# A two-layer decoder trunk on eight cores: earlier token loads, a longer prologue, another order of chunk steps, and a last group in two halves

## The chip, the cores and the metric

The kernel runs on the 8 cores of one Trainium2 chip. Every core computes one of eight batch elements, with the same program. The metric is device microseconds of the slowest core. Some executions fall into a slow state (the cores of one die at a lower granted TensorE clock, the time 2 to 19% longer in the runs here). Ratios and intervals here use fast runs alone; the medians of times in the tables are over all runs, slow ones included.

## The reference, cut to what matters

```python
def reference(x, ...):                       # x: (8, 2048, 1024) float32, one batch element a core
    for i in range(2):
        h = rmsnorm(x, norm_mix_g[i])
        x = x + (mlstm_mixer if i == 0 else gla_mixer)(h, ...)   # 4 heads, dk 128, dv 256
        h = rmsnorm(x, norm_ffn_g[i])
        x = x + square(relu(h @ w1[i])) @ w2[i]                  # 1024 -> 4096 -> 1024
    return rmsnorm(x, final_norm_g)
# mlstm_mixer: q, k, v, output gate and input/forget gates are one projection of h; a recurrence over
# chunks with a matrix state C (dk x dv a head) and a vector state n; a norm by head; a projection out.
```

## The kernel before

The tokens are on the free axis: `xT` is [128 partitions, 8 blocks of 128 features, 2048 tokens]. They are taken in four groups of 512 and sixteen chunks of 128. The program does not issue its instructions directly. It records them as units with the tiles that they read and write. A list scheduler then orders each engine's queue by a model of times, and the order that comes out is emitted. So a change of the recording order or of a dependency can move any instruction.

```python
    def order(s):                          # the scheduler, cut
        ...
        for e in s.E:                      # each engine: the unit of its window that can start first
            cand = []
            for n in todo[e][:s.WIN[e]]:
                ...                        # rdy: when its predecessors are done in the model
                st = max(free[e], rdy)
                cand.append((st, n))
```

The square sums of RMSNorm have two forms. The direct one sends each of eight squares through TensorE (eight matmuls against ones). The other one adds four squares on GpSimd first, so that TensorE gets only two matmuls a group.

```python
    def sq_half(g, hf):                    # four of the eight feature blocks of group g
        for i, k in enumerate(ks):
            act(sq[:, i % 2, :], xT[:, k, tgs(g)], AF.Square, ...)
            if i == 1:   tt(sd[:], sq[:, 0, :], sq[:, 1, :], ALU.add, ..., 512, "pool")
            elif i == 2: tt(sd[:], sd[:], sq[:, 0, :], ALU.add, ..., 512, "pool")
            elif i == 3: tt(sqb[:, hf, :], sd[:], sq[:, 1, :], ALU.add, ..., 512, "pool")

    def xn_op(layer, g, gcol, k):          # x * gain * rstd on VectorE: two operands from SBUF
        stt(XN[...], xT[:, k, tgs(g)], gains[...], rstd[:], ALU.mult, ALU.mult, ...)
```

One chunk of a mixer. S2 is the output (scores times values plus query times state), P2a to P2c the norm by head, S34 the state update, Cst the bf16 copy of the state, S7 the transposition of a chunk's result, S1 the next chunk's scores. `f()` takes one of the chunk's fills: projections of later chunks and groups, the output projection, statistics of the next group.

```python
                s.S2(i)
                s.P2a(i)
                s.S34(i, 0)
                s.S34(i, 1)
                s.Cst(i)
                f()
                if i > 0:
                    s.S7(i - 1)
                f()
                s.P2b(i)
                s.P2c(i)
```

The loads of the start and the prologue (cut):

```python
    for k0 in range(0, KC, 2):
        load_x("sp", 0, k0, 2)                      # token group 0, hardware queue
    load_cols(wqk, "wqk", m_win_d, 0, 2)            # q/k weights, cast to bf16 on the software queue
    load_z(0)                                       # weights of the input and forget gates
    load_cols(wv, "wv", m_win_d, 1024, 4)
    load_cols(wo, "wo", m_win_d, 2048, 4)
    load_x("pool", 1, 0, 8)                         # token group 1
    stats_direct(0, range(KC), MB)                  # group 0; group 1 follows in chunk 0, by GpSimd
    ...                                             # q/k of group 0, gates, values of chunks 0 to 3
    wout_load(0, 0)
    load_x("pool", 2, 0, 8)
```

The last group of the kernel is one block of 512 columns: down projection, add, square, statistics, and then eight outputs of 512 columns with their stores.

## Time and profile before

| | before |
|---|---|
| time, first four runs (one of them slow) | 1529.52 us median |
| time, all 16 runs (five of them slow) | 1529.0 us median, 1527.28 to 1671.56 |
| time, the 11 fast runs | 1528.7 us mean |
| profiled spans of the cores | 1520.0 to 1526.2 us |
| priced TensorE work | 1429.0 us |
| the rest ("excess"), slowest core | 97.2 us |

Excess is the measure of the prediction, which says how each matmul is priced: the wall time less the priced TensorE work. It rises only where TensorE stands or runs at a low clock. Where I give it for stretches below, it is the mean of the six cores whose traces are complete (cores 2 and 4 lack some matmul records, which inflates theirs).

The busy line of the page of before gives for each engine busy microseconds, share of the span, and instructions:

```profile
PE 1461.7 (96%) x7476; PEld 688.8 (45%) x7476; DVE 807.2 (53%) x1433; ACT 603.2 (40%) x1245; POOL 186.8 (12%) x173
```

The waits of TensorE in before (who waited <- who ended the wait: total us, times, longest):

```profile
PE ps L230 <- ACT sq L236: 19.9, 4, 9.0
PE ps L230 <- DVE hn L240: 7.8, 1, 7.8
PE ps L230 <- DVE R L244: 4.7, 7, 1.2
PE ps L230 <- DMA wv<-m_win: 3.3, 1, 3.3
```

These few waits hold over a third of the excess, and the change aims at them. Two groups of VectorE (line, engine, operation, tiles, shapes, count | busy us, mean ns of one | idle time before them):

```profile
L244 DVE SCALAR_TENSOR_TENSOR xn<-xT,gains,rstd 128x512 bf16<-128x512 f32 x128 | 96.2, 791 | 28.8 <-ACT rstd L236 28.7
...
L244 DVE SCALAR_TENSOR_TENSOR tiny<-tiny 128x4 f32<-128x4 f32 x32 | 7.5, 235 | 2.2 <-ACT junk L236 0.6
```

A group of GpSimd (POOL):

```profile
L240 POOL TENSOR_TENSOR sd<-sq 128x512 f32<-128x512 f32 x36 | 46.5, 1291 | 530.4 <-ACT sq L236 353.6 <-DVE NB L608 159.5 <-ACT rstd L236 17.3
```

An operation on 4 columns that means 235 ns, where its neighbours of the same size on the timeline take 160, and an xn that means 791, where an undisturbed one takes 737 to 753, are the trace of something that holds VectorE back some of the time. (The 0.69 us of the prediction is the spacing of xn in a row: two take 1.40.) The single records are plainer than the means: 10 of the 128 xn take over 0.76 us, up to 1.85, and each of these lies beside a GpSimd sum; none of the 113 that lie beside no sum does, not even the 7 beside a DMA issue of GpSimd. The timeline of before at the 7.8 us hole shows it (start us, duration us, engine, line, operation, tiles, shapes, count, idle before <- releaser):

```profile
71.08 2.80 DVE L724 TENSOR_SCALAR Cbf<-R,egs 128x256 bf16<-128x256 f32 x4
...
71.72 0.71 POOL L190 DMA_DIRECT2D wst<-m_wout  x1 [59.37 <-DVE Cbf L724]
...
72.44 1.28 POOL L240 TENSOR_TENSOR sd<-sq 128x512 f32<-128x512 f32 x1
...
74.58 1.26 POOL L240 TENSOR_TENSOR sd<-sd,sq 128x512 f32<-128x512 f32 x1 [0.86 <-ACT sq L236]
...
74.88 0.99 DVE L240 TENSOR_TENSOR n<-n,egs 128x4 f32<-128x4 f32 x1
```

Four state copies took 2.80 us here (by the single records three took 0.35 us each and the last 2.01, to 0.16 us after the end of the first sum), and a product of 4 columns 0.99 us, up to the end of a GpSimd sum that had begun 0.3 us before it.

### The profile page before, as it was taken

The page shows a single profiled execution, that of the slowest core. Times are in us where ns is not written, and L with a number is a line of the kernel's source. Part 1 is how long each engine was busy: PE and PEld are TensorE (multiplying, and loading weights), DVE is VectorE, ACT ScalarE, POOL GpSimd, SP SyncE. Part 2 cuts the span into 40 slices and gives each one's busy share as a digit, 9 for nine tenths or more (in the row PEclk, how much of TensorE's full clock was granted, in tenths as well). Part 3 has the DMA queues.
Part 4 walks back from the last instruction along what each step waited for, and adds up shares of the span by engine and source line. Part 5 has one row for each costly group of instructions (what it writes and reads, how often), then busy time and mean ns, then how long its engine had stood idle before and what let it go on. Part 6 is the DMA issues. An engine that isn't in the chain of part 4 may idle for free.

```text
span 1526.2 us, 22507 instructions; the slowest of 8 cores (1520.0 to 1526.2 us)
## 1 busy us (share of the span) xinstructions
PE 1461.7 (96%) x7476; PEld 688.8 (45%) x7476; DVE 807.2 (53%) x1433; ACT 603.2 (40%) x1245; POOL 186.8 (12%) x173
## 2 busy tenths in 40 slices
PE   4789999999999999999999999999999999999996
PEld 1345454544444444444444544444444444444442
DVE  1276563875433434434557876768743443343367
ACT  1667676663013013013255866677410310301333
POOL 2030101322000000000110201034200000000042
PEclk9989999999999999999999999999999999999998
DMA  9920000373321330330301100036430331200014
GB/s 153 262 84 1 2 1 1 56 112 56 56 35 22 56 52 4 56 56 1 55 1 56 56 1 1 1 56 95 73 55 3 54 56 21 36 1 1 1 56 166
DMA packets 35697, 72.87 MB, mean 48 GB/s; under 512 B 4336, under 2 KB 4336, under 8 KB 35584
## 3 DMA queue, kind: packets, MB, share of 16 engines
q0 software_dynamic: 29104, 60.87, 23.0%
q1 hardware_dynamic: 6480, 10.57, 2.1%
q8 instruction: 62, 1.02, 0.3%
q14 instruction: 51, 0.42, 0.1%
HBM read 109.23 MB, written 8.39 MB: 77 GB/s over the span
## 4 chain that ended last, share of the span: by engine, by line
PE 85%; DVE 4%; ACT 3%; issue 3%; DMA 3%; POOL 1%; DVEq 0%; ACTq 0%; POOLq 0%; another core or an unknown queue 0%
PE ps L230 84%; DMA wv<-m_win 3%; ACT og L236 1%; DVE oT L244 1%; PE ps L744 1%; DVE R L244 1%; POOL sd L240 1%; DVE xn L244 1%; DVE xT L240 1%; ACT hnT L236 1%; ACT sq L236 1%; ACT junk L236 0%; PE ps L633 0%; DVE ps L240 0%; POOL sqb L240 0%
## 5 line engine op out<-in xcount | busy, mean ns | idle before, releaser
L230 PE MATMUL ps<-xn,w1b 128*128 128x512 bf16 x2048 | 445.1, 379 | 0.0
L230 PE MATMUL ps<-hid,w2b 128*128 128x512 bf16 x1920 | 417.0, 379 | 0.0
L236 ACT ACTIVATE rt<-ps 128x512 f32<-128x512 f32 x256 | 152.8, 597 | 604.9 <-PE ps L230 599.4
L240 DVE TENSOR_TENSOR xT<-ps,xT 128x512 f32<-128x512 f32 x320 | 219.3, 688 | 245.9 <-PE ps L230 245.7
L230 PEld LDWEIGHTS ps<-xn,w1b 128*128 128x128 bf16 x2048 | 200.2, 98 | 239.7
L240 DVE TENSOR_TENSOR hid<-rt 128x512 bf16<-128x512 f32 x240 | 172.1, 718 | 224.1 <-ACT rt L236 223.9
L230 PEld LDWEIGHTS ps<-hid,w2b 128*128 128x128 bf16 x1920 | 187.9, 98 | 226.2
L236 ACT ACTIVATE sq<-xT 128x512 f32<-128x512 f32 (+1 forms) x160 | 96.8, 623 | 100.4 <-DVE xT L240 47.0
L230 PE MATMUL ps<-wv,xn 128*128 128x512 bf16 x512 | 120.6, 382 | 3.4 <-DMA wv<-m_win 3.3
L230 PE MATMUL ps<-wo,xn 128*128 128x512 bf16 x512 | 120.8, 384 | 1.4 <-ACT vt L236 0.6
L230 PE MATMUL ps<-xn,wqk 128*128 128x512 bf16 x512 | 118.1, 383 | 2.5 <-DVE xn L244 2.5
L230 PE MATMUL ps<-hnT,wout 128*128 128x512 bf16 x512 | 117.8, 382 | 2.0 <-ACT vt L236 2.0
L244 DVE SCALAR_TENSOR_TENSOR xn<-xT,gains,rstd 128x512 bf16<-128x512 f32 x128 | 96.2, 791 | 28.8 <-ACT rstd L236 28.7
L240 POOL TENSOR_TENSOR sd<-sq 128x512 f32<-128x512 f32 x36 | 46.5, 1291 | 530.4 <-ACT sq L236 353.6
L236 ACT ACTIVATE og<-og 128x512 f32<-128x512 f32 x128 | 80.6, 629 | 12.4 <-ACT og L236 1.5
L230 PEld LDWEIGHTS ps<-xn,wqk 128*128 128x128 bf16 x512 | 49.8, 99 | 61.4 <-issue 6.2
L230 PEld LDWEIGHTS ps<-wo,xn 128*128 128x128 bf16 x512 | 49.4, 99 | 60.7 <-issue 8.1
L230 PEld LDWEIGHTS ps<-hnT,wout 128*128 128x128 bf16 x512 | 49.1, 98 | 57.7 <-issue 5.1
L230 PEld LDWEIGHTS ps<-wv,xn 128*128 128x128 bf16 x512 | 48.8, 98 | 56.5 <-issue 6.9
L244 DVE SCALAR_TENSOR_TENSOR R<-R,egs,ps 128x256 f32<-128x256 f32 x120 | 57.2, 477 | 15.7 <-PE ps L230 9.0
L236 ACT ACTIVATE junk<-ps 128x256 bf16<-128x256 f32 x128 | 48.6, 379 | 18.7 <-DVE ps L240 6.2
L240 POOL TENSOR_TENSOR sd<-sd,sq 128x512 f32<-128x512 f32 x36 | 47.5, 1320 | 66.4 <-ACT sq L236 62.2
(121 smaller groups left out, 987.7 us busy)
## 6 DMA issues: line engine op xcount, KB each, us to landing
w1b<-w POOLq DMA_DIRECT2D x16, 1024.0 KB, 15.8
w2b<-w POOLq DMA_DIRECT2D x16, 1024.0 KB, 14.3
outT<-oT SPq DMA_DIRECT2D x16, 512.0 KB, 2.9
xT<-xT POOLq DMA_DIRECT2D x3, 2048.0 KB, 65.6
wst<-m_wout POOLq DMA_DIRECT2D x4, 1024.0 KB, 9.0
wst<-g_wout POOLq DMA_DIRECT2D x4, 1024.0 KB, 5.6
xT<-xT SPq DMA_DIRECT2D x4, 512.0 KB, 10.1
wqk<-m_win POOLq DMA_DIRECT2D x4, 512.0 KB, 19.2
```

The source lines that it names most:

```text
L230: t.op("pe", lambda e: e.matmul(out, lhsT=lhsT, rhs=rhs, start=start, stop=stop), r=r, w=w, sig=sig, ns=max(cols, 150) * (1.7 if f32 else ...
L236: t.op("act", lambda e: e.activation(out=out, in_=in_, func=func, **kw), r=r, w=w, ns=190 + 0.84 * n + (190 if acc is not None else 0))
L240: t.op(eng, lambda e: e.tensor_tensor(out=out, in0=in0, in1=in1, op=op), r=r, w=w, ns=170 + 1.03 * n if eng == "dve" else 200 + 2.2 * n)
L244: t.op("dve", lambda e: e.scalar_tensor_tensor(out=out, in0=in0, scalar=scalar, in1=in1, op0=op0, op1=op1), r=r, w=w, ns=200 + 1.07 * n)
L744: t.op("pe", lambda e, h=h, e2=e2, e8=e8: e.transpose(tpS[:, e8, :], in_=hn[:, h, e2 * 128:(e2 + 1) * 128], identity=ident[:]), r=[("hn", ...
```

## The change

The intent: TensorE has no projection to do for the first 25 us and waits for VectorE and ScalarE in the first chunks. So both first token groups are loaded ahead of the weights, more work that needs no state is done before the first chunk, group 1's normalisation leaves the first chunks, the chunk's steps are ordered so that TensorE finds something to do between the norm's steps, and the last group's statistics are hidden behind outputs of its first half.

The diff, cut to its core (the list of fills and the index arithmetic of the tail are left out):

```diff
@@ the scheduler: a queue's transfers keep their order
+                held = False
                 for n in todo[e][:s.WIN[e]]:
+                    if s.units[n]["dma"]:
+                        if held:
+                            continue
+                        held = True
@@ the fills of a chunk, first mixer: values two chunks ahead
+            v = s.v(i + 2) if i + 2 < NCH and not (s.m and i < 2) else []
+            o = s.o(i + 1) if i + 1 < NCH else []
...
@@ the steps of a chunk, first mixer only
                 s.S2(i)
                 s.P2a(i)
-                s.S34(i, 0)
-                s.S34(i, 1)
-                s.Cst(i)
-                f()
-                if i > 0:
-                    s.S7(i - 1)
-                f()
-                s.P2b(i)
-                s.P2c(i)
+                    if i > 0:
+                        s.S7(i - 1)
+                    s.S34(i, 0)
+                    s.P2b(i)
+                    s.S34(i, 1)
+                    s.P2c(i)
+                    s.Cst(i)
+                    f()
@@ loads and prologue
+    load_x("sp", 1, 0, 4)
+    load_x("sp", 1, 4, 4)
-    load_cols(wqk, "wqk", m_win_d, 0, 2)
-    load_z(0)
-    load_cols(wv, "wv", m_win_d, 1024, 4)
-    load_cols(wo, "wo", m_win_d, 2048, 4)
-    load_x("pool", 1, 0, 8)
+    load_cols(wqk, "wqk", m_win_d, 0, 2, after=[("xT", 0, 1)])
+    load_z(0, [("xT", 0, 1)])
+    load_cols(wv, "wv", m_win_d, 1024, 2, after=[("wqk", 2)])
+    load_cols(wo, "wo", m_win_d, 2048, 2, after=[("wv", 2)])
...
+    for k in range(4):
+        slab(k)                                     # q/k of group 0, six outputs
+        stats_direct(1, (2 * k, 2 * k + 1), 7)      # group 1's statistics, direct
...
+    qk1 = m0.qk(1, 0) + m0.qk(1, 1)                 # half of group 1's q/k, before the first chunk
@@ output weights later
-    hooks.setdefault(0, []).extend([(3, lambda: wout_load(0, 1))])
-    hooks.setdefault(1, []).extend([(1, lambda: wout_load(0, 2)), (5, lambda: wout_load(0, 3))])
-    hooks.setdefault(2, []).extend([(3, lambda: load_x("pool", 3, 0, 8))])
+    hooks.setdefault(0, []).extend([(4, lambda: wout_load(0, 0))])
+    hooks.setdefault(1, []).extend([(1, lambda: wout_load(0, 1)), (4, lambda: wout_load(0, 2))])
+    hooks.setdefault(2, []).extend([(1, lambda: wout_load(0, 3)), (3, lambda: load_x("pool", 3, 0, 8))])
@@ the last token group in two halves of 256 columns
+    for hf in range(2):
+        for j in range(KC):
+            ...                                     # down projection, add, square, statistics in bank 6 + hf
+        ...                                         # Ln, Exp
+        gen = out_ops(g, hf * n, n, rt[:, hf, 0:n], ("rt", hf))
```

The second mixer keeps its old fills and steps.

## The prediction

> **What bounds the kernel now.** I read the busy shares first, then busy time by stretch, then the waits of TensorE, then single holes on the timeline. TensorE is busy 96% of the span, so only its holes can be won. Busy time by stretch (columns: stretch, its length, busy time and count of PE, PEld, DVE, ACT, POOL, then granted clock, DMA share, GB/s):
>
> ```profile
> 0.00:46.00 46.00, 21.68 (x109) 8.73 (x110) 6.34 (x14) 11.33 (x21) 10.98 (x19) 1.00 0.96 155
> 46.00:92.00 46.00, 35.15 (x172) 17.14 (x170) 23.29 (x45) 28.20 (x66) 8.31 (x7) 0.78 0.72 213
> 92.00:140.00 48.00, 44.80 (x330) 24.17 (x331) 30.04 (x80) 34.62 (x86) 9.36 (x8) 1.00 0.13 45
> 140.00:190.00 50.00, 48.51 (x333) 25.83 (x332) 30.52 (x76) 34.64 (x84) 7.60 (x6) 1.00 0.01 1
> ...
> 334.00:787.00 453.00, 453.00 (x2095) 204.25 (x2092) 199.65 (x299) 100.96 (x167) 34.51 (x34) 1.00 0.25 38
> 787.00:1067.00 280.00, 275.62 (x1511) 135.98 (x1509) 207.56 (x410) 191.21 (x424) 47.90 (x41) 1.00 0.18 35
> 1067.00:1478.00 411.00, 411.00 (x1909) 186.40 (x1907) 179.12 (x256) 88.56 (x148) 25.58 (x25) 1.00 0.19 29
> ...
> 1504.00:1526.20 22.20, 10.65 (x49) 4.57 (x47) 13.88 (x21) 6.12 (x10) 0.00 (x0) 0.79 0.50 189
> ```
>
> The reader is to see that the feed-forward stretches are full, and that the start, the first 90 us and the tail are not. Three single holes, from the timeline:
>
> ```profile
> 25.31 15.58 PE L230 MATMUL ps<-xn,wqk 128*128 128x512 bf16 x64 [2.53 <-DVE xn L244]
> ...
> 45.81 1.86 PE L230 MATMUL ps<-wv,xn 128*128 128x512 bf16 x4 [3.25 <-DMA wv<-m_win]
> ...
> 78.05 0.37 PE L230 MATMUL ps<-vt,St 128*128 128x256 bf16 x1 [7.82 <-DVE hn L240]
> ```
>
> No projection runs before 25.3 us, although TensorE could; the value weights come late; and chunk 1 waits 7.8 us for DVE, which in program order still held other work (weight scaling, state copies, while ACT was computing the next group's squares). After that hole the clock is low (stretches of 5 us):
>
> ```profile
> 75.00:80.00 5.00, 1.95 (x10) 1.39 (x11) 2.85 (x4) 3.44 (x8) 3.38 (x3) 0.50 0.75 290
> 80.00:85.00 5.00, 3.12 (x18) 1.64 (x17) 4.11 (x9) 3.45 (x12) 2.53 (x2) 0.50 0.05 20
> 85.00:90.00 5.00, 4.59 (x15) 1.66 (x13) 4.80 (x8) 2.08 (x4) 0.00 (x0) 0.50 0.00 0
> ```
>
> Busy time counts such slow matmuls as work, so I priced each matmul by its start-to-start time in the full stretches (16 of 512 columns take 3.46 us there: 216 ns each; 256 columns 109 ns; 128 columns 56 ns; at least 25 ns), summed, and call the rest of the wall time excess. The sum is 1429 us, so the excess is 97 us: 30.4 up to the first chunk's output matmul at 64.6 us, 20.1 from there to that of chunk 4 at 126.1 us, 15.4 on to 334 us, 2.8 in the first feed-forward, 14.9 in the second mixer, 0 in the second feed-forward, 13.7 in the tail. The second mixer is not touched: the listing of both kernels' orders shows the same TensorE order from the first feed-forward to the last group. So 66 + 14 us is all the change can attack.
>
> **What the Trainium skill says.** "TensorE: Matmul & The Clock Gate", Part 1: an idle TensorE falls to half clock, and some 3.4 us of sustained work bring it back. The trace agrees: granted clock 0.50 after the 7.8 us hole, and weight loads 0.43 us apart at 85 to 88 us against 0.216. The page's table of specifications also says that ScalarE and VectorE take their queues in strict order; the hole at 78 us is such a case. "DMA: Bandwidth & Descriptors", Specifications, gives about 358 GB/s of HBM per core. The trace has 340 GB/s at 60 to 65 us with uncast loads; weights cast to bf16 on the way show half their HBM bytes, so 150 to 186 GB/s there is nearly the same limit. The same page's section on queues says an engine takes turns between queues; here the x loads of one queue land at 6.8, 9.0, 14.9 and 20.7 us once the wqk loads of the other queue join.
>
> **The change part by part.**
> *Loads.* x group 0 and then x group 1 go first, on one queue; wqk waits until half of group 1 has landed. Both kernels keep the DMA engines full (share 0.96), so this only reorders bytes. At the 1.5 to 2.2 us between the first two 0.5 MB landings, x0 is in at about 12 us instead of 20.7, and x1 by about 19 instead of 65.6. wqk then needs 4 MB at 3.4 us each (its landings at 20.2, 23.8, 27.0): last one about 33.5, against 27.0 before. The gate weights take about 4 us (27.0 to 31.5): 37. wv takes 14 us (31.5 to 45.7): 51 against 45.7. wo another 14: 65 against 59.7. So the weights come 5 to 6 us later, and x1 46 us earlier.
> *TensorE at the start.* The q/k slabs of six outputs follow wqk and end near 36.5 us (two slabs are 2.6 us after the last landing). Then the fourth head 3.5, gates twice 2.2, and half of group 1's q/k (32 matmuls, 6.9): 49. The values then wait about 1.5 us for wv, take 13.8 us: 64.5; output gate 3.5: first chunk at about 68 instead of 64.6. But 9.5 us more is done by then (6.9 q/k, 0.9 gates, 1.7 stats), of which 1.3 us is extra work, since direct statistics take 8 matmuls where sums made on POOL take 2. Excess at this point about 24.5 instead of 30.4.
> *First four chunks.* Group 1's squares, sums and eight xn operations (8 x 0.69 us of DVE) are gone from here. Per chunk DVE keeps about 8.4 us (two products 1.4, small ones 1.5, four R 1.9, four Cbf 1.7, two hn 1.4, St 0.7) and 1.5 for scaling wout; ACT about 10; TensorE has 2.5 of recurrence and 6.9 of fills (q/k of heads 2 and 3, values, gates), 9.5. Three engines nearly level: I expect 10 to 11 us a chunk and 3 to 6 us of excess in place of 20.1. Chunk 4 then starts near 109 us with one more value block (3.5 us) done: 20 us gained so far, of which the start is 5.
> *Later chunks of the first mixer.* Transposing the last chunk's result now stands before the state update, and the normalisation between its two halves. By hand, the second half still waits 0.2 to 0.5 us for DVE to empty its bank, some 12 times. Excess 8 to 10 instead of 15.4: gain 6.
> *Tail.* The last group is cut in two halves of 256 columns. TensorE work is the same. Before, from the last down matmul (1513.7) to the end are 12.5 us: add, square, sum, Ln, Exp (3.6 us with their gaps, 1513.95 to 1517.58), eight outputs 5.4, and 3.1 from the last issue (1523.0) to landing. Afterwards the same five steps are 256 wide (about 2.5 us), hidden by the first half's eight outputs (about 0.41 us each, 3.3), then eight more, 3.3. The order listing shows all 16 outputs behind the last add, because adds and outputs share a key for the whole group; so the overlap wanted is only partial. Gain 1.5 us.
> Sum: 20 + 6 + 1.5 = 27.5, up to 31 if x arrives at the quicker rate. With fast runs before at about 1529: 1500.
>
> **The rivals.**
> A, the loads cancel the gain: wqk, wv and wo come 5 us later, and if the x loads or the small transfers cost more than I took, the first chunk starts at 72 rather than 68; gain 22, 1507. For it: DMA share 0.96 from the start. Against it: no byte is added, and TensorE now has 9 us of other work while it waits.
> B, DVE or ACT become the bound of the first four chunks, since all three engines are within 10% there and the wout scaling waits in order for loads that now come behind wo and x2 (about 74 us): chunks of 12 to 13 us, gain 20, 1509. For it: DVE's order stood in the way at 78 us before. Against it: 8 squares and 8 xn have left.
> C, the new order removes nearly all waits of the first mixer, and x lands at the 1.5 us pace: start 8, chunks 16, later 10, tail 2 to 3: gain 37, 1492.
> D, nothing gained, because TensorE is 96% busy. Against it: the 97 us, counted above.
>
> **Range and chances.** I take 1500. A and B together give 1510 as the upper end of 8 in 10, C with a little less gives 1490. The line for 2% is about 1498, inside the range and almost at the middle: faster by over 2% 0.44, within 2% 0.54, slower by over 2% 0.02 (that needs weights so late that the whole start stalls).
>
> **What would show it.** Right: first chunk's output matmul at 66 to 70 us, chunk 4's at 105 to 112; no wait of TensorE over 2 us between 45 and 300 us, and granted clock 1.00 at 75 to 90; wqk landing last at 32 to 35 us; the stretches from 334 on of equal length; the tail from the last down matmul about 11 us. Wrong: a DMA wait of several us before the values or the output gate (A); DVE or ACT busy all through 70 to 110 with TensorE waiting (B); a second mixer of another length, which I hold to be untouched.

## The result, and the profile after

| | before | after |
|---|---|---|
| time, median of all runs | 1529.0 us (16 runs) | 1504.89 us (11 runs, 1503.12 to 1795.41) |
| time, mean of fast runs | 1528.7 us (11 runs) | 1504.8 us (8 runs) |
| ratio of fast runs, 95% interval | 1 | 0.9844, 0.9834 to 0.9854 |
| profiled spans of the cores | 1520.0 to 1526.2 us | 1497.1 to 1502.7 us |
| mean granted clock, medians of the two dies | 0.992, 0.992 | 0.998, 0.998 |
| priced TensorE work | 1429.0 us | 1430.4 us |

The kernel is 1.6% faster, so "within 2%" is the class that came, and 1504.9 lies in the range of 1490 to 1510. A ratio is the mean time of one kernel's fast runs over the mean of the other kernel's fast runs of the same rounds, so it is not quite the ratio of the medians in the tables.

The busy line of after:

```profile
PE 1458.6 (97%) x7554; PEld 694.3 (46%) x7554; DVE 806.7 (54%) x1449; ACT 604.3 (40%) x1255; POOL 180.7 (12%) x170
```

It hardly differs; no engine's work changed by much. Busy time by stretch of after (columns as in the prediction; the long stretches are set to the same stages):

```profile
0.00:46.00 46.00, 28.70 (x131) 11.17 (x132) 11.97 (x24) 18.01 (x35) 9.67 (x19) 1.00 0.94 177
46.00:92.00 46.00, 45.01 (x313) 24.19 (x312) 20.75 (x58) 32.52 (x80) 3.73 (x5) 1.00 0.65 153
92.00:140.00 48.00, 44.28 (x313) 24.63 (x312) 36.87 (x90) 38.30 (x90) 9.23 (x8) 1.00 0.26 83
140.00:190.00 50.00, 48.08 (x319) 24.81 (x317) 23.75 (x63) 33.93 (x84) 7.60 (x6) 1.00 0.01 1
310.00:763.00 453.00, 453.00 (x2092) 204.24 (x2091) 203.69 (x304) 100.94 (x168) 33.84 (x34) 1.00 0.23 38
763.00:1043.00 280.00, 276.00 (x1508) 135.97 (x1507) 206.18 (x410) 192.08 (x425) 49.42 (x42) 1.00 0.17 34
...
1480.50:1502.70 22.20, 13.17 (x109) 10.08 (x106) 16.58 (x38) 7.89 (x22) 1.25 (x1) 0.89 0.59 204
75.00:80.00 5.00, 5.00 (x43) 3.11 (x42) 4.66 (x10) 4.64 (x10) 0.72 (x1) 1.00 0.01 3
80.00:85.00 5.00, 4.93 (x34) 2.66 (x33) 4.43 (x15) 4.17 (x13) 0.00 (x0) 1.00 0.61 211
```

From 0 to 92 us TensorE is busy for 73.7 us at a granted clock of 1.00 where before it was busy for 56.8, some of it at half clock. The feed-forward and second-mixer stretches have the same length and the same busy time. Single places on the timeline of after, which answer to the three holes of the prediction:

```profile
25.76 16.15 PE L235 MATMUL ps<-xn,wqk 128*128 128x512 bf16 x64 [2.99 <-DVE xn L249]
...
50.99 5.34 PE L235 MATMUL ps<-wv,xn 128*128 128x512 bf16 x24
...
78.03 0.27 PE L235 MATMUL ps<-vt,St 128*128 128x256 bf16 x1
```

The first projection begins no earlier than before (25.8 against 25.3 us), but the 64 matmuls after it are followed by other work until the value weights are there, without a wait at 51 us, and chunk 1 begins at 78.0 without a hole. The waits of TensorE that are left:

```profile
PE ps L235 <- ACT sq L241: 15.0, 6, 9.4
PE ps L235 <- ACT tiny L241: 5.4, 7, 1.3
PE ps L235 <- DVE R L249: 4.3, 8, 1.8
PE ps L235 <- DVE xn L249: 3.0, 1, 3.0
PE ps L638 <- DVE R L249: 2.2, 1, 2.2
```

9.4 us of the first line are the wait for the first tokens, and the waits for hn and for wv have gone. The waits for R, which is VectorE emptying the bank of the state update, are no shorter than before: 4.3 and 2.2 us against 4.7 and 1.4. Excess by stretch (us, mean of six cores; chunks are counted at their first output matmul; the first feed-forward lies between chunk 15 and the second mixer's first chunk):

| stretch | before | after | predicted for after (from the profiled core) |
|---|---|---|---|
| up to chunk 0 | 30.1 | 25.1 | 24.5 |
| chunks 0 to 4 | 19.8 | 2.0 | 3 to 6 |
| chunks 4 to 15 | 13.8 | 13.3 | 8 to 10, with the next line |
| chunk 15 to the second mixer | 3.5 | 3.0 | |
| second mixer to the end | 28.8 | 26.3 | 1.5 less |
| sum | 96.1 | 69.7 | |

So 26.4 us of excess went, 1.4 us of matmul work came (the direct statistics of group 1), and 25.0 us are left, where 23.8 were timed (1528.7 to 1504.8, means of the fast runs; the time is that of the slowest core, the excess a mean of six). The start and the first four chunks brought all that was predicted of them, and the tail a little more. The later chunks of the first mixer, from which 6 us were expected, gave 1.0. (Their 15.4 us before is one core's, from chunk 4 to 334 us; over that same stretch the profiled cores gained some 1.2.)

By chunk the picture is uneven (same means). Chunks 0 and 1 went from 8.5 and 10.4 us to 0.9 and 0.2. Chunks 4 to 13 together went from 10.3 to 7.8, and chunk 14 alone from 3.4 to 5.4.

### The profile page after: what moved, and what is told of

Same layout as the page of the kernel before. It is cut to its first block, busy times and chain, and to the rows that moved or that the text cites. A ratio compares the mean times of both kernels' runs of the same rounds, so it can differ in the third digit from the quotient of the medians.

```text
span 1502.7 us, 22750 instructions; the slowest of 8 cores (1497.1 to 1502.7 us)
## 1 busy us (share of the span) xinstructions
PE 1458.6 (97%) x7554; PEld 694.3 (46%) x7554; DVE 806.7 (54%) x1449; ACT 604.3 (40%) x1255; POOL 180.7 (12%) x170
## 4 chain that ended last, share of the span: by engine, by line
PE 92%; DVE 3%; DMA 2%; issue 2%; ACT 1%; SPq 0%; DVEq 0%; ACTq 0%; POOLq 0%
PE ps L235 91%; DMA xT<-xT 1%; DMA wst<-m_wout 1%; PE ps L749 1%; DVE R L249 1%; PE ps L638 0%; DVE ps L245 0%; ACT hnT L241 0%; DVE oT L249 0%; ACT junk L241 0%; SPq L195 0%; DVE xn L249 0%; DVE wout L426 0%; DVE Cbf L729 0%; DMA outT<-oT 0%
## 5 line engine op out<-in xcount | busy, mean ns | idle before, releaser
L235 PE MATMUL ps<-hid,w2b 128*128 128x512 bf16 (+1 forms) x1984 | 417.8, 372 | 0.9 <-DVE xT L245 0.7
L245 DVE TENSOR_TENSOR xT<-ps,xT 128x512 f32<-128x512 f32 (+1 forms) x328 | 220.0, 675 | 246.5 <-PE ps L235 246.1
L235 PEld LDWEIGHTS ps<-hid,w2b 128*128 128x128 bf16 x1984 | 193.7, 98 | 222.1 <-issue 1.6
L241 ACT ACTIVATE sq<-xT 128x512 f32<-128x512 f32 (+2 forms) x168 | 96.6, 602 | 86.1 <-DVE xT L245 42.5
## 6 DMA issues: line engine op xcount, KB each, us to landing
w2b<-w POOLq DMA_DIRECT2D x16, 1024.0 KB, 12.3
```

The costliest lines, as they stand in the source:

```text
L235: t.op("pe", lambda e: e.matmul(out, lhsT=lhsT, rhs=rhs, start=start, stop=stop), r=r, w=w, sig=sig, ns=max(cols, 150) * (1.7 if f32 else ...
L241: t.op("act", lambda e: e.activation(out=out, in_=in_, func=func, **kw), r=r, w=w, ns=190 + 0.84 * n + (190 if acc is not None else 0))
L245: t.op(eng, lambda e: e.tensor_tensor(out=out, in0=in0, in1=in1, op=op), r=r, w=w, ns=170 + 1.03 * n if eng == "dve" else 200 + 2.2 * n)
```

## The experiments

Two questions: which part of the change brings which part of the 24 us, and why the later chunks did not follow. My first theory was that the later chunks are held by GpSimd's square sums, which stop VectorE, whatever the order of the steps; its rival that the new order did bring a gain there and something else took it back. All kernels gave correct results but the one told below. Each was run beside before; chips differ between the batches, so I compare ratios to before, and excess by stretch. The scheduler can answer an edit with another order: by their traces pool_tiny and x3_wait keep the order of all matmuls of after, tail_old changes it in the tail alone, and the others move some.

| run | time us | ratio, 95% interval | to 0 | 0 to 4 | 4 to 15 | 15 to 16 | to end |
|---|---|---|---|---|---|---|---|
| before | 1529.0 | 1 | 30.1 | 19.8 | 13.8 | 3.5 | 28.8 |
| after | 1504.89 | 0.9844 (0.9834 to 0.9854) | 25.1 | 2.0 | 13.3 | 3.0 | 26.3 |
| order_old | 1507.43 | 0.9864 (0.9846 to 0.9881) | 24.6 | 2.4 | 14.9 | 5.5 | 26.2 |
| ungated | 1510.84 | 0.9882 (0.9864 to 0.9900) | 30.6 | 1.8 | 14.7 | 3.0 | 26.3 |
| qk1_late | 1509.92 | 0.9880 (0.9858 to 0.9902) | 30.4 | 1.7 | 13.1 | 3.4 | 26.7 |
| pool_tiny | 1495.51 | 0.9780 (0.9760 to 0.9801) | 24.3 | 1.7 | 7.3 | 2.8 | 23.7 |
| tail_old | 1508.24 | 0.9869 (0.9852 to 0.9885) | 25.9 | 2.2 | 13.7 | 3.0 | 28.2 |
| held_off | 1530.56 | 1.0013 (0.9997 to 1.0030) | 45.9 | 4.3 | 15.4 | 3.3 | 26.8 |
| x3_wait | 1505.37 | 0.9843 (0.9824 to 0.9863) | 25.4 | 2.2 | 12.3 | 3.0 | 26.0 |
| dve_sum | 1496.00 | 0.9787 (0.9773 to 0.9802) | 24.5 | 2.5 | 6.6 | 4.1 | 23.6 |
| dve_order_old | 1502.47 | 0.9799 (0.9741 to 0.9856) | 24.6 | 2.8 | 9.4 | 3.7 | 23.6 |
| before_dve | 1512.77 | 0.9886 (0.9829 to 0.9942) | 29.9 | 12.3 | 7.6 | 3.6 | 25.7 |
| before_held | 1529.32 | 0.9989 (0.9932 to 1.0046) | 30.6 | 21.8 | 12.2 | 3.5 | 28.5 |
| dve_m1 | 1494.22 | 0.9762 (0.9706 to 0.9817) | 23.7 | 1.9 | 6.5 | 4.1 | 22.5 |

The last five columns are excess in us by the chunks of the table above; their sum and the 1429.0 or 1430.4 us of work give a core's span. In the last batch one run of before at 1547 us counts as fast, which widens the four last intervals and makes their ratios 0.0016 too small (2.4 us) beside the other batches.

### order_old: the old steps of a chunk in the changed kernel

```diff
-                if s.m:
-                    ...                 # S7, S34(0), P2b, S34(1), P2c, Cst
-                else:
+                if True:
                     s.S34(i, 0)
```

> The changed kernel with one part undone: inside a chunk of the first mixer the old sequence of steps (both halves of the state update, then the transposes, then the normalisation). Theory 1 (from comparing the traces: excess from chunk 4 to chunk 15 was 14.6 us before and 14.4 after): the new sequence brings nothing there; 1503 to 1507 us, excess of chunks 4 to 15 13 to 15 us, of chunks 0 to 4 within 1.5 us of the changed kernel's 2 to 4. Theory 2: the new sequence is what emptied the first four chunks; their excess goes back to 8 us or more and the time to 1509 to 1513.

Measured 1507.43 us, about 3 us slower than the changed kernel by the ratios (0.9864 to 0.9844), with intervals that overlap a little. The excess is 1.6 us more in chunks 4 to 15 and 2.5 us more after them; the first four chunks do not change. Theory 2 is out; theory 1 has the excess right (14.9 in its 13 to 15), but "brings nothing" is not so, and neither theory foresaw the 2.5 us after chunk 15. So the order is worth 3 to 4 us inside the changed kernel, but the changed kernel with the old order is 1.1 us worse than before in chunks 4 to 15 and 2.0 us worse after them (14.9 and 5.5 against 13.8 and 3.5): the rest of the change took most of the order's gain beforehand. What of the rest does it, the new fills or something else, I did not separate.

### ungated: the q/k weights do not wait for the tokens

```diff
-    load_cols(wqk, "wqk", m_win_d, 0, 2, after=[("xT", 0, 1)])
-    load_z(0, [("xT", 0, 1)])
+    load_cols(wqk, "wqk", m_win_d, 0, 2)
+    load_z(0)
```

> The changed kernel, but the q/k and gate weights do not wait for half of x group 1. Theory 1 (the DMA engines are full either way, so bytes are only reordered): last q/k weights land at 33 to 36 us as with the wait (35.2), first chunk's output matmul at 67 to 70 us, time 1503 to 1507. Theory 2 (the two queues take turns and slow each other, as x did before): x group 0 lands after 18 us and group 1 after 27, first chunk 3 us or more later, 1508 to 1512.

Measured 1510.84 us, and the start's excess is 30.6 us, as in before. The second theory was right, and the first missed. In the trace token group 0 had landed at 25.4 us instead of 13.9, group 1 at 35.0 instead of 19.7, and the last q/k piece at 30.0 instead of 35.2: the two queues share the engines by turns, and the first projection, which needs the whole of group 0, waits for the slower of the two. The timeline of this run:

```profile
29.92 2.72 PE L235 MATMUL ps<-xn,wqk 128*128 128x512 bf16 x6 [2.41 <-DVE xn L249]
```

It starts 4.2 us later than the 25.76 of after, though three of the four weight pieces had been there since 25.0.

### qk1_late: half of group 1's q/k back in chunks 0 and 1

```diff
-    qk1 = m0.qk(1, 0) + m0.qk(1, 1)     # and its four calls between the gates
...
-                    return x[:2] + o + x[2:] + v + (qk(2) if s.m else [])
+                    return x[:2] + o + x[2:] + v + (qk(2) + qk(0) if s.m else [])
...
-                        return o + qk(3)
+                        return o + qk(3) + qk(1)
```

> The changed kernel, but the q/k projections of group 1, heads 0 and 1 (32 matmuls, 6.9 us) go back from the start into chunks 0 and 1. Theory 1 (the start waits for loads: the output-gate weights land at 64 us and need 3.5 us of matmuls after that, so there is no earlier first chunk than 67.7 us): the first chunk comes at 66 to 68 us, not earlier, and chunk 4 about 6 us later; 1509 to 1512. Theory 2 (the start is bound by TensorE's work): first chunk at 62 us, chunk 4 unchanged, 1503 to 1507.

Measured 1509.92 us. The first chunk comes at 65.3 to 72.8 us, hardly earlier than the 66.7 to 72.0 of after, though 6.9 us of work had left the time before it. The start is bound by the loads, and q/k work put there is free: without it 5.3 us of excess come back (30.4 against 25.1). The first theory was right.

### pool_tiny: the GpSimd sums on 8 of 512 columns (a wrong result, on purpose)

```diff
-                tt(sd[:], sq[:, 0, :], sq[:, 1, :], ALU.add, ..., 512, "pool")
+                tt(sd[:, 0:8], sq[:, 0, 0:8], sq[:, 1, 0:8], ALU.add, ..., 512, "pool")
...                                      # the same for the other two; the fourth square goes
...                                      # straight to TensorE and is scaled by 4
```

> Wrong result on purpose (statistics from a quarter of the channels, scaled by 4): the sums of squares on GpSimd touch 8 columns instead of 512; TensorE and VectorE keep exactly the order of the changed kernel. Theory 1: GpSimd's 1.3 us operations hold an SBUF port that VectorE operations with two SBUF inputs need, so xn takes up to 1.7 us instead of 0.69 and state updates come late; without them xn has a mean under 700 ns (814 in the changed kernel), the excess of chunks 4 to 15 falls from 14.4 us to 6 to 9, and the time to 1494 to 1500. Theory 2: the waits there come from the chunk's own chain; excess stays 12 us or more, time 1502 to 1506.

The result is off by 0.10, as it must be. TensorE and VectorE keep their order, and only GpSimd's sums take 0.2 us instead of 1.3. Measured 1495.51 us, some 10 us faster than the changed kernel by the ratios. Chunks 4 to 15 have 7.3 us of excess instead of 13.3. The first theory was right in time; its detail of an xn below 700 ns on average missed, since 744 is what an undisturbed xn takes, as this group of its trace shows:

```profile
L249 DVE SCALAR_TENSOR_TENSOR xn<-xT,gains,rstd 128x512 bf16<-128x512 f32 x128 | 89.8, 744 | 20.3 <-ACT rstd L241 20.3
...
L249 DVE SCALAR_TENSOR_TENSOR tiny<-tiny 128x4 f32<-128x4 f32 x32 | 5.1, 160 | 3.0 <-ACT junk L241 1.2
```

The same groups of after:

```profile
L249 DVE SCALAR_TENSOR_TENSOR xn<-xT,gains,rstd 128x512 bf16<-128x512 f32 x128 | 98.8, 814 | 22.4 <-ACT rstd L241 22.4
...
L249 DVE SCALAR_TENSOR_TENSOR tiny<-tiny 128x4 f32<-128x4 f32 x32 | 6.9, 214 | 2.3 <-ACT junk L241 0.5
```

Of the 128 xn of after, 12 take over 0.76 us, up to 1.87, each beside a sum; of the 110 beside none, 10 of them beside a DMA issue of GpSimd, not one does. How little VectorE time becomes much TensorE time is seen in chunk 14 of after, on its timeline:

```profile
277.05 1.27 POOL L245 TENSOR_TENSOR sd<-sq 128x512 f32<-128x512 f32 x1 [0.93 <-ACT sq L241]
...
277.19 2.33 DVE L249 SCALAR_TENSOR_TENSOR xn<-xT,gains,rstd 128x512 bf16<-128x512 f32 x2
...
280.86 1.25 POOL L245 TENSOR_TENSOR sqb<-sd,sq 128x512 bf16<-128x512 f32 x1 [0.21 <-ACT junk L241]
...
281.18 0.96 DVE L249 SCALAR_TENSOR_TENSOR tiny<-tiny 128x4 f32<-128x4 f32 x1
...
281.21 0.24 PE L235 MATMUL ps<-ubf,ktok 128*128 128x1 bf16 x4 [1.00 <-DVE tiny L249]
...
282.06 1.06 DVE L249 SCALAR_TENSOR_TENSOR R<-R,egs,ps 128x256 f32<-128x256 f32 x2
...
283.27 0.58 PE L235 MATMUL ps<-vt,ktok 128*128 128x256 bf16 x2 [1.82 <-DVE R L249]
```

The two xn, which take 1.40 us in the same place of pool_tiny, take 2.33 beside a sum. The product of 4 columns begins 0.3 us after the next sum and ends where that sum ends. R stands behind it in VectorE's queue, and TensorE's second state matmuls stand behind R. The answering lines of pool_tiny:

```profile
275.08 1.40 DVE L249 SCALAR_TENSOR_TENSOR xn<-xT,gains,rstd 128x512 bf16<-128x512 f32 x2
...
278.31 0.22 POOL L245 TENSOR_TENSOR sd<-sd,sq 128x8 f32<-128x8 f32 x1
...
278.77 0.16 DVE L249 SCALAR_TENSOR_TENSOR tiny<-tiny 128x4 f32<-128x4 f32 x1
```

In chunks 12 to 15 the profiled core of after has three such holes that dve_sum (below) does not have: 1.25 us at 267.2, 1.17 at 281.2 and 1.96 at 283.3. Behind the last, six matmuls in a row begin 0.43 us apart instead of 0.216, 1.3 us more, at a granted clock of 0.50. Together they make 5.7 us of the 6.5 by which the two kernels' excess from chunk 12 to 15 differs on these cores (8.5 and 2.0).

This is the sharing of ports that the Trainium skill describes in "SBUF — State Buffer", under "Who interferes with whom": a VectorE instruction with two SBUF inputs contends with a GpSimd instruction that reads SBUF, and the contention is an exclusive lock. The trace agrees: xn, tiny and n have two SBUF inputs and are held until a 1.3 us sum has ended; R, which has one of its large inputs in PSUM, takes 478 ns on average with and without the sums.

### tail_old: the last group as one block again

```diff
-    g, n = NG - 1, GS // 2
-    for hf in range(2):
-        ...
+        if g == NG - 1:
+            for _ in gen:
+                pass
+            rstd_fin(MB)
```

> The changed kernel with the old tail (last group as one block of 512 columns, one set of statistics, eight outputs after it). Theory 1 (the halves are worth about what was predicted, because the first half's outputs cover the second half's statistics): 1.5 to 3 us slower than the changed kernel, 1506.5 to 1508, and the time from the last down-projection matmul to the end 1.5 to 3 us longer, with nothing else moved. Theory 2 (the tail is bound by VectorE and the landing of the last output, so halves bring nothing): within 0.7 us of 1505. Theory 3 (the halves carry most of the 2.4 us and more that I found after the second mixer began, and the second mixer gained nothing): over 3 us slower.

Measured 1508.24 us. From the start of the last down-projection matmul to the end of the kernel it takes 13.1 us (mean of the eight cores) against 10.1 with the halves and 12.9 in before; the excess after the second mixer's start is 1.9 us more. The time differs by 3.8 us by the ratios, of which the start of this run's slowest core accounts for some: there the first chunk came at 75.1 us, without any edit there. I take 2 to 3 us for the halves, the upper end of the first theory. The timeline of after shows the cover at work: the first half's eight outputs lie over the second half's Ln and Exp.

```profile
1493.42 3.24 DVE L249 SCALAR_TENSOR_TENSOR oT<-xT,gains,rt 128x256 f32<-128x256 f32 x8
...
1494.71 0.38 ACT L241 ACTIVATE sd<-ps 128x256 f32<-128x256 f32 x1 [0.51 <-PE ps L235]
...
1495.19 0.42 ACT L241 ACTIVATE rt<-sd 128x256 f32<-128x256 f32 x1
...
1496.93 3.44 DVE L249 SCALAR_TENSOR_TENSOR oT<-xT,gains,rt 128x256 f32<-128x256 f32 x8 [0.27 <-DMA outT<-oT]
```

The prediction gave as the reason for the partial overlap that adds and outputs share a key for the whole group. That all 16 outputs come behind the last add is so in the trace (1493.42 after 1493.07); the overlap is full all the same. I built a version with separate keys by half, whose listing was the same, so the keys do not seem to be the reason; it was not run.

### held_off: the scheduler's old rule in the changed kernel

```diff
                     if s.units[n]["dma"]:
-                        if held:
-                            continue
                         held = True
```

> The changed kernel with the old rule of the scheduler, which lets a later transfer pass an earlier one that waits for its predecessor in the model. In the built listing the software queue then has token groups 2 and 3 and the first piece of the output weights (5 MB) ahead of the q/k weights, and pieces of the output weights between those of the value and gate weights. Theory 1 (the start is bound by the order of bytes): the last q/k weight lands about 15 us later than 35.2 (5 MB at 340 GB/s), the first chunk's output matmul comes 10 to 18 us later than 67 to 72, and the time is 1512 to 1522. Theory 2 (the rule only cleans up the model; the queue has slack): 1504 to 1507 and the same first chunk.

Measured 1530.56 us: no gain is left. The direction was the first theory's and the size was not. The last q/k piece landed at 53.9 us instead of 35.2, token group 0 at 19.8 instead of 13.9, and the first half of group 1, by which the q/k weights are gated, at 29.3 instead of 16.8, because token groups 2 and 3 and a piece of the output weights, which wait for nothing, go out on the other queue at once. I had counted the 5 MB ahead of the weights (15 us) and not that they also delay those tokens. The first chunk comes at 82.5 to 90.4 us. TensorE's waits in this run:

```profile
30.20 2.14 PE L233 MATMUL ps<-sq,ones_bf 128*128 128x512 bf16 x4 [8.32 <-ACT sq L239]
36.32 2.14 PE L233 MATMUL ps<-sq,ones_bf 128*128 128x512 bf16 x4 [3.98 <-ACT sq L239]
43.10 6.64 PE L233 MATMUL ps<-xn,wqk 128*128 128x512 bf16 x24 [4.64 <-DMA wqk<-m_win]
```

### before_held: the scheduler's new rule alone

```diff
+                    if s.units[n]["dma"]:
+                        if held:
+                            continue
+                        held = True
```

> The kernel before with the new rule of the scheduler alone (a queue's transfers keep their order in the model). In the built listing it only moves the load of token group 3 behind two pieces of output weights. Theory 1 (the rule matters because the changed kernel makes loads wait; alone it is worth little): 1526 to 1531. Theory 2 (the rule is a gain of its own): below 1522.

Measured 1529.32 us, no different from before; the first theory was right. (Its trace shows more than the moved load: 68 matmuls of chunks 1 and 2 come in another order.) Alone the rule is worth nothing, and the change without it is worth nothing either. They are a pair: the new waits of the loads create the gaps in the model into which the old rule lets later loads slip.

### x3_wait: token group 3 waits for the output weights

```diff
-                                   (3, lambda: load_x("pool", 3, 0, 8))])
+                                   (3, lambda: load_x("pool", 3, 0, 8, [("wout", 6)]))])
```

> The changed kernel, but the load of token group 3 waits until the fourth pair of output weights has been scaled; TensorE, VectorE and ScalarE keep their order. Theory 1 (on the slower cores the third piece of output weights lands at about 104 us because it shares the engines with token group 3, and VectorE, which takes its queue in order, stands at it and holds the state update): the third piece lands 2 to 4 us earlier on those cores, the hole of TensorE at 104 to 107 us shrinks, time 1 to 3 us less: 1502 to 1504. Theory 2 (the hole is VectorE's own order, or the wait is made up later): within 0.7 us of 1505.

Rival B of the prediction named a wait of the output weights' scaling. It is there on some cores (2.4 and 2.0 us of excess between chunks 3 and 4 on cores 5 and 2, 0 to 0.5 on the others); the timeline of after on core 5:

```profile
104.68 1.42 DVE L426 TENSOR_SCALAR wout<-wst,ong 128x1024 bf16<-128x1024 f32 x2 [2.75 <-DMA wst<-m_wout]
...
107.22 0.38 PE L638 MATMUL ps<-ident,kx 128*128 128x128 bf16 x4 [2.22 <-DVE R L249]
```

With the edit this wait is gone on the same core (and core 0 of that run has 4.0 us of excess in the same chunk), and the excess from chunk 6 to 8 falls by 1.0 us on all cores. But the time, 1505.37 us (1500.23 to 1508.26), is the same: in the profiled run the slowest core is the one whose first chunk came last (74.8 us), and 1 us does not show beside that. The second theory was right about the time; the hole moved to another core rather than vanish.

### dve_sum: a correct kernel without sums on GpSimd

```diff
-            act(sq[:, i % 2, :], xT[:, k, tgs(g)], AF.Square, ..., 512)
-            ...                                        # three f32 sums on GpSimd
+            act(sq16[:, i, :], xT[:, k, tgs(g)], AF.Square, ..., 512)      # squares in bf16
+            if i % 2 == 1:
+                addb(sq16[:, i - 1, :], sq16[:, i - 1, :], sq16[:, i, :], ...)   # VectorE
+        addb(sqb[:, hf, :], sq16[:, 0, :], sq16[:, 2, :], ...)
```

> A correct kernel in which no sum of squares is left on GpSimd: the squares are written as bf16 and three bf16 additions per half are done by VectorE. Theory 1 (the GpSimd sums hold back VectorE operations that read two operands from SBUF, and this costs the 9 us that the version with tiny sums won): xn operations at 0.67 to 0.75 us instead of 0.81; VectorE gets 6 additions a group (0.3 to 0.5 us each by my estimate from the 0.69 us of the f32 forms, 2 to 3 us a group over 17 groups) of which only those in the mixers matter; time 1497 to 1503. Theory 2 (VectorE is the level engine of the mixers, so that 2 to 3 us of new work a group eats what the clash gives back): 1503 to 1508.

Measured 1496.00 us, ratio 0.9787, and correct. The first theory was right, the time 1 us under its range. The groups of VectorE:

```profile
L249 DVE SCALAR_TENSOR_TENSOR xn<-xT,gains,rstd 128x512 bf16<-128x512 f32 x128 | 89.9, 744 | 22.0 <-ACT rstd L241 22.0
...
L446 DVE TENSOR_TENSOR sq<-sq 128x512 bf16<-128x512 bf16 x68 | 27.9, 419 | 16.9 <-ACT sq L241 15.4 <-ACT sm L241 1.4
```

VectorE now does 43 us more of additions (68 of 419 and 34 of 422 ns), the kernel is 9 us faster, and VectorE's busy time only went from 806.7 to 816.0, because the operations that had been held gave time back: 33 us by this sum, 26 by pool_tiny, which adds nothing and where it is 780.3. The Trainium skill says in "VectorE: DVE Perf Modes", section "The perf-mode tier table", that a bf16 `tensor_tensor` in SBUF runs at twice the f32 rate (its figures, for 2048 elements, are 1224 and 2293 ns); here a 128x512 addition takes 0.42 us in bf16, against 0.69 for an f32 product of that size (`hid`, undisturbed), a factor of 1.6.

### before_dve: the kernel before with the sums on VectorE

The same edit in the kernel before.

> The kernel before with nothing changed but the sums of squares, which VectorE does in bf16. Theory 1 (the clash was there before the change as well, and its cost adds to that of loads and start): 7 to 10 us faster than before, 1518 to 1521, xn operations at about 0.74 us. Theory 2 (the clash matters only where the new sequence has put VectorE on the path of TensorE): under 4 us, 1524 or more.

Measured 1512.77 us: 15.6 us faster than before by the medians (14.6 by the means of fast runs without that of 1547 us), more than either theory said. Some three fifths of the whole change's gain are had by this edit alone. In the profile (core 0) the four state copies of the 7.8 us hole are short again:

```profile
73.28 1.14 DVE L724 TENSOR_SCALAR Cbf<-R,egs 128x256 bf16<-128x256 f32 x4
```

The excess falls by 7.5 us in chunks 0 to 4, by 6.2 in chunks 4 to 15, and by 3.1 after the second mixer's start. The first of these was part of what the change had removed, since group 1's GpSimd sums leave chunk 0 there; the second it had not touched. The sums are not alone in this: the scheduler also moved some 340 of the 7476 matmuls, most of them in chunks 1, 2, 14 and 15, and I did not separate the two. Nor is the first gain even: chunk 1 falls from 10.4 to 0.3 us, and chunk 0 rises from 8.5 to 11.5. In chunk 14 the excess is 3.4 us in before and 0.1 here, 5.4 in after, 2.3 in pool_tiny and 1.0 in dve_sum: most of what the sums cost the later chunks lies there.

### dve_order_old: does the order matter without the sums?

The edit of order_old on dve_sum.

> The kernel with the sums of squares on VectorE (1496.0 us), with the old sequence of a chunk's steps in the first mixer. With the sums on GpSimd the old sequence cost 2.5 us in time. Theory 1 (the new sequence has a small gain of its own, about 2 us in chunks 8 to 12 and the last chunk, whatever the sums do): 1497.5 to 1500, excess of chunks 4 to 15 of 8 to 10 us instead of 6.7. Theory 2 (the prediction's gain of 6 us is there once the sums no longer hold VectorE back; the clash only hid it): 1501 to 1504, excess of chunks 4 to 15 above 11 us.

The fast runs are 1497.5, 1502.6, 1496.6 and 1502.3 us, two by two; their mean is 4 us above that of dve_sum. The excess of chunks 4 to 15 is 9.4 us against 6.6, and the sum 64.2 against 61.3. By the excess the first theory was right (8 to 10); the mean time lies at its upper end. The order's gain is about 3 us without the sums, against 3 to 4 with them. It was not hidden by them.

### dve_m1: the new steps in the second mixer too

```diff
-                if s.m:
+                if True:
                     if i > 0:
                         s.S7(i - 1)
```

> The kernel with the sums of squares on VectorE, with the new sequence of a chunk's steps in the second mixer too; meant as a version that beats both kernels. Theory 1 (a transposition ahead of the state update saves the second mixer about what it saved the first in its quiet chunks 8 to 12, 0.5 us a chunk): 3 to 7 us less than 1496.0, 1489 to 1493. Theory 2 (the second mixer's holes are elsewhere, at ScalarE's logarithm and exponential of a chunk's norm): 1495 to 1498.

Measured 1494.22 us (1492.58 to 1495.63), ratio 0.9762. That is between the two theories, 1.5 us less than the mean of dve_sum, run on another chip, so this last step is small and not sure; the excess after the second mixer's start went from 23.6 to 22.5. It is the fastest of the correct kernels, 2.4% below before (2.2% without the run of 1547 us) and 0.7% below the changed one.

## Why the prediction was right or wrong

*The start* (excess 24.5 predicted, 25.1 measured; 25.0 on the profiled core): right, by the steps given, with two errors that cancel: the last q/k piece came 1.7 us late, and the gate weights took 1.1 us after it and not 4. First chunk at 68 us: 68.7 on the profiled core, 66.7 to 72.0 over the cores. Token group 0 at 12 us: 13.9; group 1 at 19: 19.7; last q/k piece at 33.5: 35.2; last value piece at 51: 49.95; last output-gate piece at 65: 64.2. That both parts are needed, tokens first and work to fill the wait, is shown by ungated and qk1_late: each takes back 5.3 to 5.5 us. The scheduler's rule, of which the prediction says nothing, is what makes the order of the loads hold (held_off).

*The first four chunks* (3 to 6 predicted; 3.8 on the profiled core, 2.0 on average): right in size on that core; on average the gain was larger than predicted. The reason was incomplete. The prediction counts ScalarE's squares, the xn operations and VectorE's queue; in before_dve 7.5 of the 19.8 us go when the sums leave GpSimd. Which part of the change took the rest is not shown: this is the largest gain of all, and no run puts group 1's normalisation or the old fills back. order_old shows only that it was not the order of the steps.

*The later chunks* ("Excess 8 to 10 instead of 15.4: gain 6"): wrong, and the term that was mis-sized. On average 17.3 us (13.8 and 3.5) became 16.3. The step that failed is the count of waits behind the 8 to 10: "the second half still waits 0.2 to 0.5 us for DVE to empty its bank, some 12 times". Counting gaps of over 0.15 us before a matmul in chunks 4 to 15 of the profiled cores, the state matmuls have 9 of them with 5.7 us in after (mean 0.63, up to 2.0), and 8 with 4.8 in before; in dve_sum they have 5 with 1.5, and there the 0.3 us each that I had reckoned is right. The new order did take something away, the gaps before the output projection (3.0 us before, 0.8 after), but gave back 0.9 at the state matmuls, 1.2 before the product for the vector state and 0.7 at a low clock behind a long hole. So the quoted wait, some 4 us by its own figures, was too small by 1 to 2 us only; the rest of the miss is in what the count left out. Two things stand in the place of the 6 us. First, some 6 of the 13 to 14 us of chunks 4 to 15 belong to the GpSimd sums, and this order of the steps did not touch them. For after this is shown: pool_tiny, with the same order of matmuls, has 7.3 of the 13.3. For before it is 6.2 by before_dve (7.6 of 13.8), where the order moved as well. Second, of the 7.6 that the order could reach it took 2.8 (dve_order_old to dve_sum), of which 1.8 had been lost to another part of the change (9.4 against 7.6), a net of 1.0. So even without the sums the term would have been 1 and not 6: the sums explain why so much was left, not why the order brought so little. What loses the 1.8 is open. Whether the sums' cost is all lock, or partly that their results came late, pool_tiny and dve_sum do not separate for the whole kernel, since in both the sums are also done sooner; in before ScalarE, too, waits for sums, 28 times and 36 us in all, of which 4.7 in chunks 4 to 15 of the profiled core. For chunks 12 to 15 of after the three holes named above all end with VectorE, not with a sum.

*The tail* (1.5 predicted): 2 to 3 us. The mechanism was right; the overlap, called partial, was full: the outputs of the first half cover the second half's Ln and Exp.

*Second mixer and feed-forward untouched*: right (stretches of equal length, 275.6 and 276.0 us of TensorE in 280).

*The rivals.* A did not come: the loads were 1 to 2 us off. B came in a small form, one wait of 2.2 us at 107 on the slower cores. C asked for later chunks at 10 and was wrong there. D was wrong. Of the signs, "no wait of TensorE over 2 us between 45 and 300" failed by that one wait, and the clock was 1.00 at 75 to 90 as said.

*The sum*: 20 + 6 + 1.5 = 27.5 predicted. Measured 21.4 for start and first chunks (5.0 + 17.8 less 1.4 of work), 1.0, and 2.5: 24.9, and 23.8 timed. The 27.5 from 1529 give 1501.5; the 1500 leans to the "up to 31". The later chunks fell short by 5 us, and the start, first chunks and tail together gave 2.4 more than predicted, so the total came nearer than its terms. Both 1500 and 1504.9 lie on the same side of the 2% line (1498). One small slip: the items of VectorE's 8.4 us a chunk add up to 8.6.

## What to carry to other kernels

Before pricing a new order of steps, compare the mean duration of each small VectorE operation with its shortest: where the mean lies well above it (235 against 160 ns here), look at the long ones singly and at what another engine does beside them (12 long xn of 128 in after, all beside a GpSimd sum), before counting on an order of its own queue. Reordering loads pays when the work that waits for them is reordered as well, and only if the thing that decides the final order, here a scheduler's model, is made to keep it. A part that does nothing alone (the rule here) can still carry the whole gain of the others.

## What the Trainium skill lacked or had wrong

- "SBUF — State Buffer", "Who interferes with whom": the rule of the exclusive lock is stated and agrees with the places shown here. What it lacks is the size that this takes in a kernel: operations of 4 columns at 0.96 to 0.99 us instead of 0.16, one f32 to bf16 `tensor_scalar` copy at 2.01 us instead of 0.35, and some 10 us of 1505 (pool_tiny, the order of matmuls unchanged) from sums that occupy GpSimd for 9% of the span.
- "DMA: Bandwidth & Descriptors", "Queues, rings and completion order": the engines' turns between queues are stated. It has no number for what a second queue does to a load that others wait for: token group 0 landed at 25.4 us (ungated) and 19.8 (held_off) instead of 13.9.
- No page says how far the eight cores of one program lie apart at the start: first chunk at 66.7 to 72.0 us in one execution of the changed kernel, 65.6 to 75.1 in one of tail_old, which hides gains of 1 us.
